# One decoder layer on one core: half a dense block more beside the first attention head, 640 keys cut as 320 and 320, and a norm's sum in two float32r parts

## The chip, the cores and the metric

The kernel runs on one core of a Trainium2 chip. The metric is device time of one execution in microseconds (us). The core has five engines with queues of their own: PE (TensorE, matrix products), DVE (VectorE), ACT (ScalarE), POOL (GpSimd) and SP, which here only issues DMAs. Each engine takes its instructions in program order and waits for others by semaphores.

## The reference

One layer of a decoder trunk on 1024 tokens of width 1024, all in float32:

```
u = rms_norm(h);  aq, ak, av, hq, hf, hi, hg = split(u @ w_in)
attn = rms_norm(dilated_attention(aq, ak, av))        # 8 heads of 64
rec  = rms_norm(hgrn2_mixer(hq, hf, hi)) * silu(hg)   # 4 heads of 128
h = h + concat(attn, rec) @ w_out
h = h + conv_glu(rms_norm(h));  return rms_norm(h)
```

The attention's three dilated branches are merged into one softmax by a mask that carries the logarithm of how many branches contain a pair of tokens. So a block of 128 queries at block number qb sees (qb + 1) * 128 keys, from 128 to 1024.

## The kernel before

**Numbers.** A float32 product is made of float32r parts: each operand is split into a high part (`hi`, a cast on ACT, L86 for weights) and the rest (`lo`, a subtraction, L88, on POOL or DVE), and PE makes three products, hi·hi, hi·lo and lo·hi. In the attention the weights' `lo` parts are made on POOL.

**Stages.** The projections of the first heads come first. Then the attention's eight heads run from about 50 to 298 us, the recurrent heads until about 500, then the output projection, the gated network and the last norm.

**One attention head.** Query blocks go in four pairs j = 0 to 3. `score_steps` makes the scores S of a block (L585, L586: q against the keys' high and low parts) in pieces of at most 512 keys, one per step. DVE adds the mask and takes the extreme (L588), with one more small operation where there are two pieces (L592). ACT takes the exponential (L593, tile P), DVE the reciprocal of its sum (L594), and POOL scales P by it, 512 columns at a time (L597). `value_steps` then transposes P on PE (L612 to L619, tile T), ACT and DVE split the result (L623, L624, tiles th and tl), and PE multiplies it with the values (L631 to L635, tile O; L639 and L641 add the two halves). The scores of pair j+1 are made while pair j is transposed, and the last pair of a head goes with the first pair of the next.

**S has two banks** (tag `s`). The third piece in a row may be written only once DVE has read the first.

**Fill.** Between these steps stand steps of other projections, so that PE has work while softmax goes through DVE, ACT and POOL. A step is three products: 512 columns wide for the queries and keys of a later head (`qk_half`, tile `p__qk_h_half`, eight steps each, L458 to L461) and for the recurrent part's tokens (`tok_pair`, tile piv, sixteen steps), 256 wide for values (tiles pV, L475 to L477 and L492 to L494). The list `beside[h]` names what stands beside head h. `cost[h]`/4 is the fill in planned us for each pair, shared evenly between its steps. What is left is run at the end of the head:

```python
share = cost[h] / 4 / (n_sc + n_va)
...
if got:
    fill.run(share)
```

PE's order is written out this way by hand. On DVE, ACT and POOL a scheduler sets the order when the program is built.

**Weights.** `Ring` holds five loaded weight pairs. `ring.done(key)` after a pair's last use frees a slot for the next pair's cast on ACT and its `lo` part on POOL. A projection of one query/key half uses two pairs, and the second half uses the same two and frees them. A value projection uses four.

**Attention norm.** `attn_norm` squares the heads' outputs and adds them in `acc` (L821 to L824), then sums over the partitions with a product against ones. This one is in plain float32:

```python
yield
ss = bank("t", f"ass{hf}")
PE.matmul(ss, ones, acc, start=True, stop=True)
R = rstd_part(acc, s2, ss, 1.0 / 512)
```

It runs twice, once for each half of the tokens, two units of the recurrent part's plan (5.2 planned us each) behind the squares. The norms before and after the gated network already use `parts_of` (ACT makes hi, DVE makes lo) and `sum_parts` (two float32r products, L344).

Of the kernel before, what the change touches and what calls it, by code (L numbers as in the profile page):

```python
# [14 lines left out]
ALU = mybir.AluOpType  # L15
# [6 lines left out]
H2 = 512  # L22
NH = 8
# [179 lines left out]
def hybrid_kernel(ctx: ExitStack, tc: tile.TileContext, xT, w_qk, w_tok, w_hg, w_out, w_up,  # L203
                  w_down, vecs, amask, hmask, out):
    nc = tc.nc
    PE, DVE, ACT, POOL = nc.tensor, nc.vector, nc.scalar, nc.gpsimd
# [128 lines left out]
    def parts_of(x, tile):  # L335

        hi, lo = tile("hi"), tile("lo")
        ACT.copy(hi, x)
        DVE.tensor_sub(lo, x, f32(hi))
        return hi, lo  # L340
# [142 lines left out]
    def two(kind, i, evac):  # L483

        key = f"{kind}_{i}"
        for e in range(2):
            o = bank("mm", f"p{key}_{e}")[:, :256]
            tk = slice((2 * i + e) * P, (2 * i + e + 1) * P)
            for c in range(NCT):
                hi, lo = ring.get((key, c // 2))  # L490
                s = slice((c % 2) * 256, (c % 2 + 1) * 256)
                PE.matmul(o, uhi[:, c, tk], hi[:, s], start=(c == 0), stop=False)  # L492
                PE.matmul(o, uhi[:, c, tk], lo[:, s], start=False, stop=False)
                PE.matmul(o, ulo[:, c, tk], hi[:, s], start=False, stop=(c == NCT - 1))  # L494
                if e and c % 2 == 1:
                    ring.done((key, c // 2))
                yield 0.33
            evac(2 * i + e, o)

    def tok_pair(i, evac, lag=2):  # L500

        ps = {}
        for k in range(NCT + lag):
            for e in range(2):
                c = k - e * lag
                if not 0 <= c < NCT:
                    continue
                if c == 0:
                    ps[e] = bank("mm", f"piv{i}_{e}")
                hi, lo = ring.get((("iv", i), c))  # L510
                tk = slice((2 * i + e) * P, (2 * i + e + 1) * P)
                PE.matmul(ps[e], uhi[:, c, tk], hi, start=(c == 0), stop=False)  # L512
                PE.matmul(ps[e], uhi[:, c, tk], lo, start=False, stop=False)  # L513
                PE.matmul(ps[e], ulo[:, c, tk], hi, start=False, stop=(c == NCT - 1))  # L514
                if e:
                    ring.done((("iv", i), c))
                yield 0.65
                if c == NCT - 1:
                    evac(2 * i + e, ps[e])
# [7 lines left out]
    if True:  # L527
# [30 lines left out]
        def qk_block(h):  # L558
            return [qk_half(h, 0, False), qk_half(h, 1, True)]

        def v_evac(g):
            def evac(t, ps):
                if g not in vs:
                    vs[g] = vtile([P, 8, 4, P], F32R, f"v{g}")
                dst = vs[g][:, t]
                src = ps[:, :256].rearrange("p (h e) -> p h e", h=4)
                ACT.mul(dst[:, :, 0:64], src, R1T[:, t : t + 1])
                DVE.scalar_tensor_tensor(dst[:, :, 64:128], src, R1T[:, t : t + 1], f32(dst[:, :, 0:64]),
                                         op0=ALU.mult, op1=ALU.subtract)
            return evac  # L570

        def score_steps(h, j):
            Ps = []
            qs, kh, kl = qk[h]
            for i in range(2):
                qb = 2 * j + i
                n = (qb + 1) * P
                Pt = at.tile([P, (5 + i + 2 * (j % 2)) * P], F32, tag=f"P{j % 2}{i}", name=f"P{h}_{qb}")
                st = at.tile([P, 16], F32, tag="st", name=f"st{h}_{qb}", bufs=8)
                Ps.append(Pt)  # L580
                for k0 in range(0, n, H2):
                    w = min(n, k0 + H2) - k0
                    S = bank("s", f"S{h}_{qb}_{k0}")
                    q = qs[:, qb * P : (qb + 1) * P]
                    PE.matmul(S[:, :w], q, kh[:, k0 : k0 + w], start=True, stop=False)  # L585
                    PE.matmul(S[:, :w], q, kl[:, k0 : k0 + w], start=False, stop=True)  # L586
                    m = SEQ - n + k0
                    DVE.tensor_tensor_reduce(Pt[:, k0 : k0 + w], S[:, :w], mask[:, m : m + w], -1.0, BIG * 3,  # L588
                                             op0=ALU.add, op1=ALU.min, accum_out=st[:, k0 // H2 : k0 // H2 + 1])
                    if k0 + w == n:  # L590
                        if k0:
                            DVE.tensor_tensor(st[:, 0:1], st[:, 0:1], st[:, 1:2], op=ALU.min)  # L592
                        ACT.activation(Pt[:, :n], Pt[:, :n], AF.Exp, bias=st[:, 0:1], scale=-1.0, accum_out=st[:, 2:3])  # L593
                        DVE.reciprocal(st[:, 3:4], st[:, 2:3])  # L594
                        for s0 in range(0, n, H2):
                            e = Pt[:, s0 : min(n, s0 + H2)]
                            POOL.tensor_scalar(e, e, st[:, 3:4], 1.0, op0=ALU.mult, op1=ALU.mult)  # L597
                    yield Ps
# [100 lines left out]
        for c in range(4):  # L699
# [2 lines left out]
        fill.add(v0[4])  # L702
        fill.run()
        ivs = [tok_pair(i, iv_evac) for i in range(4)]
        beside = {
            0: v0[5:] + [two("V1", 0, v_evac(1))],
            1: qk_block(2) + [two("V1", 1, v_evac(1))],
            2: qk_block(3) + [two("V1", 2, v_evac(1))],
            3: qk_block(4) + [two("V1", 3, v_evac(1))],
            4: qk_block(5) + [islice(ivs[0], 8)],  # L710
            5: [ivs[0]] + qk_block(6) + [islice(ivs[1], 8)],
            6: [ivs[1]] + qk_block(7) + [islice(ivs[2], 8)],
            7: [ivs[2], ivs[3]],
        }
        cost = {h: 4.8 * (4 if h in (5, 6) else 3) for h in range(NH)}
        cost[NH - 1] = 12.8
        for h in range(NH):
            fill.add(*beside[h])
# [46 lines left out]
    with pool("hg", "right") as hg:  # L765
# [52 lines left out]
        def attn_norm(hf):  # L818
            t = halves[hf]
            acc, s2 = gtile(f"asq{hf}"), gtile(f"asq{hf}_s")  # L820
            ACT.activation(acc, raw[0, hf], AF.Square)  # L821
            for c in range(1, 4):
                ACT.activation(s2, raw[c, hf], AF.Square)
                DVE.tensor_add(acc, acc, s2)  # L824
            yield
            ss = bank("t", f"ass{hf}")
            PE.matmul(ss, ones, acc, start=True, stop=True)
            R = rstd_part(acc, s2, ss, 1.0 / 512)
            yield
            for c in range(4):  # L830
                if c == 2:
                    yield
                a = raw[c, hf]
                DVE.scalar_tensor_tensor(a, a, col(V_AG + c), R, op0=ALU.mult, op1=ALU.mult)
                ACT.copy(attn_hi[:, c, t], a)
                DVE.tensor_sub(attn_lo[:, c, t], a, f32(attn_hi[:, c, t]))
            yield
# [695 lines left out]
```

## Time and profile before

| | |
|---|---|
| runs, us | 1208.57, 1209.03, 3102.54 |
| median, us | 1209.03 |
| profiled execution, us | 1207.86 |
| its span, first to last instruction, us | 1205.9 |
| granted TensorE clock, mean share of full speed | 0.998 |
| busy, share of the span: PE, PEld, DVE, ACT, POOL | 99%, 83%, 79%, 52%, 25% |

PE's busy time is modelled from pipelined products, so a busy PE may still lose some tenths of a us. How long a product really takes is read as the distance from one start to the next. One of the three runs stands far from the others, and the median does not hang on it.

### The profile page before, as it was taken

Reading aid. Unit: us, or ns where it says so; the run is one execution under the profiler, and the core shown is the slowest. Engines: PE = TensorE matmul, PEld = TensorE weight load, DVE = VectorE, ACT = ScalarE, POOL = GpSimd, SP = SyncE. Lnnn points to the kernel's source line nnn. Section 1 sums busy time; section 2 is a strip of 40 time slices with the busy share of each in tenths; the row PEclk is TensorE's granted clock in tenths of the full one; section 3 lists DMA queues with packets and bytes.
Section 4 is the critical chain, followed back from the end, with each engine's and each line's share of the span. In section 5 each row is a group of like instructions: output and inputs, shape, how many; then the busy total and the mean of one; then the engine's idle time right before and its main releaser. Section 6 shows DMA issues by size and latency. Waiting matters only on the chain.

```text
span 1205.9 us, 17474 instructions
## 1 busy us (share of the span) xinstructions
PE 1192.7 (99%) x6014; PEld 1005.6 (83%) x6014; DVE 947.8 (79%) x1783; ACT 631.4 (52%) x1217; POOL 298.5 (25%) x276
## 2 busy tenths in 40 slices
PE   9999999999999999999999999999999999999996
PEld 8988888888888888888888888888888888888886
DVE  8767776666778776484999899898888978957986
ACT  8766666667666565454643343433443444444553
POOL 1154446544001014413231322312223200000000
PEclk9999999999999999999999999999999999999999
DMA  7021112223111123432113323333223267534532
GB/s 273 10 71 54 53 54 88 64 65 120 36 36 54 60 64 112 133 125 94 42 64 114 108 85 106 121 116 109 84 98 122 96 213 249 156 98 158 166 103 89
DMA packets 71833, 122.39 MB, mean 101 GB/s; under 512 B 7360, under 2 KB 17856, under 8 KB 71744
## 3 DMA queue, kind: packets, MB, share of 16 engines
q1 hardware_dynamic: 60528, 101.41, 26.3%
q10 hardware_dynamic: 11216, 19.86, 4.3%
q8 instruction: 47, 0.77, 0.3%
q14 instruction: 42, 0.34, 0.1%
HBM read 97.65 MB, written 23.59 MB: 101 GB/s over the span
## 4 chain that ended last, share of the span: by engine, by line
PE 95%; DVE 3%; ACT 1%; issue 0%; POOL 0%; DVEq 0%; ACTq 0%
PE p L1132 11%; PE p L1133 11%; PE p L1134 11%; PE ds L1433 3%; PE ds L1431 3%; PE ds L1432 3%; PE po L1036 2%; PE po L1038 2%; PE po L1037 2%; PE da L1433 2%; PE da L1431 2%; PE da L1432 2%; PE piv L512 1%; PE piv L514 1%; PE piv L513 1%; PE S L585 1%
## 5 line engine op out<-in xcount | busy, mean ns | idle before, releaser
L88 POOL TENSOR_TENSOR wlo<-raww,whi 128x512 fp32r<-128x512 f32 x141 | 208.6, 1491 | 382.4 <-ACT whi L86 231.6
L86 ACT CAST whi<-raww 128x512 fp32r<-128x512 f32 x276 | 167.7, 617 | 183.9 <-DVE raww L120 69.1
L88 DVE TENSOR_TENSOR wlo<-raww,whi 128x512 fp32r<-128x512 f32 x136 | 97.5, 717 | 22.8 <-ACT whi L86 22.7
L86 ACT CAST whi<-r 128x512 fp32r<-128x512 f32 x70 | 43.6, 623 | 83.1 <-PE ds L1432 51.3
L597 POOL TENSOR_SCALAR P<-P,st 128x512 f32<-128x512 f32 (+2 forms) x96 | 55.8, 592 | 107.9 <-DVE st L594 50.5
L588 DVE CUSTOM_DVE_ANT_0 P<-S,mask 128x512 f32<-128x512 f32 (+2 forms) x96 | 52.0, 553 | 29.9 <-PE S L586 28.9
L593 ACT ACTIVATE P<-P,st 128x128 f32<-128x128 f32 (+3 forms) x64 | 49.7, 777 | 32.0 <-DVE st L588 16.7
L88 DVE TENSOR_TENSOR wlo<-r,whi 128x512 fp32r<-128x512 f32 x70 | 47.9, 685 | 20.0 <-ACT whi L86 19.9
L624 DVE TENSOR_TENSOR tl<-T,th 128x512 fp32r<-128x512 f32 (+1 forms) x80 | 50.8, 634 | 16.2 <-ACT th L623 15.1
L1433 PE MATMUL ds<-fhi,wlo 128*128 128x512 f32 x160 | 62.3, 389 | 0.0
L1432 PE MATMUL ds<-flo,whi 128*128 128x512 f32 x160 | 62.3, 389 | 0.0
L1431 PE MATMUL ds<-fhi,whi 128*128 128x512 f32 x160 | 62.2, 389 | 0.0
L1132 PE MATMUL p<-b1h,whi 128*128 128x512 f32 x160 | 62.2, 389 | 0.0
L1133 PE MATMUL p<-b1l,whi 128*128 128x512 f32 x160 | 62.2, 389 | 0.0
L1134 PE MATMUL p<-b1h,wlo 128*128 128x512 f32 x160 | 62.2, 389 | 0.0
L1161 ACT ACTIVATE cv<-cv 128x512 f32<-128x512 f32 x44 | 27.9, 633 | 61.5 <-DVE cv L1154 61.4
L1154 DVE SCALAR_TENSOR_TENSOR cv<-g,vec,cv 128x511 f32<-128x511 f32 (+2 forms) x92 | 56.1, 615 | 4.7 <-ACT cv L1151 3.7
L1405 POOL TENSOR_TENSOR facc<-facc,sqf 128x256 f32<-128x256 f32 x2 | 1.5, 738 | 223.7 <-ACT sqf L1404 223.7
L623 ACT CAST th<-T 128x512 fp32r<-128x512 f32 (+1 forms) x80 | 43.0, 537 | 23.4 <-PE T L616 20.3
L86 ACT CAST fhi<-rawf 128x512 fp32r<-128x512 f32 x70 | 43.2, 617 | 15.2 <-DMA rawf<-spT 7.0
L88 DVE TENSOR_TENSOR flo<-rawf,fhi 128x512 fp32r<-128x512 f32 x70 | 47.9, 684 | 3.6 <-ACT fhi L86 3.6
L1431 PE MATMUL da<-fhi,whi 128*128 128x512 f32 x120 | 46.7, 389 | 0.0
(672 smaller groups left out, 3832.5 us busy)
## 6 DMA issues: line engine op xcount, KB each, us to landing
raww<-in_w_up_dram SPq DMA_DIRECT2D x88, 256.0 KB, 3.1
raww<-in_w_tok_dram SPq DMA_DIRECT2D x52, 256.0 KB, 2.7
rawf<-spT SPq DMA_DIRECT2D x40, 256.0 KB, 2.7
r<-in_w_down_dram SPq DMA_DIRECT2D x40, 256.0 KB, 3.5
raww<-in_w_hg_dram SPq DMA_DIRECT2D x32, 256.0 KB, 2.6
raww<-in_w_out_dram SPq DMA_DIRECT2D x32, 256.0 KB, 2.6
spB<-a ACTq DMA_DIRECT2D x30, 256.0 KB, 2.2
spT<-t ACTq DMA_DIRECT2D x30, 256.0 KB, 2.0
```

The costliest lines, as they stand in the source:

```text
L86: self.pin(self.high(hi[:, :w], raw))
L88: self.pin(low.tensor_sub(lo[:, :w], raw, f32(hi[:, :w])))
L588: DVE.tensor_tensor_reduce(Pt[:, k0 : k0 + w], S[:, :w], mask[:, m : m + w], -1.0, BIG * 3, op0=ALU.add, op1=ALU.min, accum_out=st[:, k0 / ...
L597: POOL.tensor_scalar(e, e, st[:, 3:4], 1.0, op0=ALU.mult, op1=ALU.mult)
L624: DVE.tensor_sub(tl[:, :n], T[:, :n], f32(th[:, :n]))
L1132: PE.matmul(ps, hi[:, s], bhi, start=(start and n == 0), stop=False)
L1133: PE.matmul(ps, hi[:, s], blo, start=False, stop=False)
L1134: PE.matmul(ps, lo[:, s], bhi, start=False, stop=(stop and n == len(rhs) - 1))
L1154: DVE.scalar_tensor_tensor(dst, x, col(V_CW + j * NFF + f), dst, op0=ALU.mult, op1=ALU.add)
L1431: PE.matmul(ps[d], hi[:, s], ahi, start=(k == 0), stop=False)
L1432: PE.matmul(ps[d], hi[:, s], alo, start=False, stop=False)
L1433: PE.matmul(ps[d], lo[:, s], ahi, start=False, stop=(k == NPAIR - 1))
```

## The change

Three edits.

1. A block with 640 keys was cut in 512 and 128. It is now cut in 320 and 320 (`cut`). Every head has one such block (qb = 4).
2. `beside` is shifted by half a query/key block from head 0 to head 4. Head 0 gets the first half of head 2's block, and heads 1 to 3 run the second half of one block, a value projection and the first half of the next block. Head 4 gets the second half of head 5's block and the whole first token pair. Head 5 loses what head 0 won (half a token pair's place), so that from head 6 on all stands as before. The sequence of the fill is the same as before. What changes is which score and value steps it stands between. Head 0's planned cost goes from 14.4 to 17.3 us, head 5's from 19.2 to 14.4.
3. `attn_norm` makes high and low parts of `acc`, in the not yet used space of `attn_hi` and `attn_lo`, and sums these with two float32r products.

```diff
-                for k0 in range(0, n, H2):
-                    w = min(n, k0 + H2) - k0
+                cut = 320 if n == 640 else H2
+                for k0 in range(0, n, cut):
+                    w = min(n, k0 + cut) - k0
...
-            0: v0[5:] + [two("V1", 0, v_evac(1))],
-            1: qk_block(2) + [two("V1", 1, v_evac(1))],
+            0: v0[5:] + [two("V1", 0, v_evac(1)), blocks[2][0]],
+            1: [blocks[2][1], two("V1", 1, v_evac(1)), blocks[3][0]],
...
-        cost = {h: 4.8 * (4 if h in (5, 6) else 3) for h in range(NH)}
+        cost = {h: 4.8 * {0: 3.6, 6: 4}.get(h, 3) for h in range(NH)}
...
+
+            parts = parts_of(acc, lambda x: (attn_hi if x == "hi" else attn_lo)[:, 0, t])
             yield
             ss = bank("t", f"ass{hf}")
-            PE.matmul(ss, ones, acc, start=True, stop=True)
+            sum_parts(ss, parts)
```

What this does to the order of instructions is shown at three places.

POOL in head 0, pairs 1 and 2, before and then with the change. P_4 to P_7 are the softmax blocks, wlo the low parts of weights; a block's number stands behind its name, and the last number is the buffer's.

```order
L597 TENSOR_SCALAR P_4_659<-P_4_659,st_4_660 128x512
L597 TENSOR_SCALAR P_4_659<-P_4_659,st_4_660 128x128
L88 TENSOR_TENSOR wlo_751<-raww_748,whi_750 128x512
L597 TENSOR_SCALAR P_5_703<-P_5_703,st_5_704 128x512
L597 TENSOR_SCALAR P_5_703<-P_5_703,st_5_704 128x256
L88 TENSOR_TENSOR wlo_781<-raww_778,whi_780 128x512
```

```order
L598 TENSOR_SCALAR P_4_662<-P_4_662,st_4_663 128x512
L598 TENSOR_SCALAR P_4_662<-P_4_662,st_4_663 128x128
L88 TENSOR_TENSOR wlo_739<-raww_736,whi_738 128x512
L88 TENSOR_TENSOR wlo_759<-raww_756,whi_758 128x512
L88 TENSOR_TENSOR wlo_775<-raww_772,whi_774 128x512
L598 TENSOR_SCALAR P_5_709<-P_5_709,st_5_710 128x512
L598 TENSOR_SCALAR P_5_709<-P_5_709,st_5_710 128x256
```

Three low parts instead of one now stand between block 4 and block 5.

ACT at the same place, before and then with the change: exponentials (L593, then L594), casts of weights (whi), casts of transposed blocks (th), a value projection's result (v) and the copy of O (ot).

```order
L593 ACTIVATE P_4_659,st_4_660<-P_4_659,st_4_660 128x640
L623 CAST th_1_1_728<-T_1_1_724 128x384
L567 ACTIVATE v_436<-pV_6_655,R1T 128x4x64
L639 COPY ot_0_754<-O_0_638 64x256
L86 CAST whi_750<-raww_748 128x512
L593 ACTIVATE P_5_703,st_5_704<-P_5_703,st_5_704 128x768
L86 CAST whi_780<-raww_778 128x512
```

```order
L594 ACTIVATE P_4_662,st_4_663<-P_4_662,st_4_663 128x640
L567 ACTIVATE v_436<-pV_6_655,R1T 128x4x64
L86 CAST whi_738<-raww_736 128x512
L624 CAST th_1_1_749<-T_1_1_745 128x384
L86 CAST whi_758<-raww_756 128x512
L640 COPY ot_0_778<-O_0_641 64x256
L594 ACTIVATE P_5_709,st_5_710<-P_5_709,st_5_710 128x768
L86 CAST whi_774<-raww_772 128x512
```

Two weight casts instead of one stand ahead of block 5's exponential, and the third cast, which POOL's third low part needs, stands behind it.

PE in head 1, from block 6's second piece of scores to block 7's first, before and then with the change.

```order
L586 MATMUL S_6_512_1171<-kl_206,qs_319 128x384
L458 MATMUL p__qk___2_1_1115<-uhi,whi_945 128x512
L460 MATMUL p__qk___2_1_1115<-ulo,whi_945 128x512
L461 MATMUL p__qk___2_1_1115<-uhi,wlo_946 128x512
L612 MATMUL T_2_0_1184<-ident,P_4_1069 128x128
L613 MATMUL T_2_0_1184<-ident,P_5_1100 128x128
L615 MATMUL T_2_0_1184<-ident,P_4_1069 128x128
L616 MATMUL T_2_0_1184<-ident,P_5_1100 128x128
L585 MATMUL S_7_0_1195<-kh_320,qs_319 128x512
```

```order
L587 MATMUL S_6_512_1221<-kl_206,qs_319 128x384
L492 MATMUL pV_1_1_1232<-whi_925,uhi 128x256
L493 MATMUL pV_1_1_1232<-wlo_926,uhi 128x256
L494 MATMUL pV_1_1_1232<-whi_925,ulo 128x256
L613 MATMUL T_2_0_1237<-ident,P_4_1109 128x128
L614 MATMUL T_2_0_1237<-ident,P_5_1146 128x128
L616 MATMUL T_2_0_1237<-ident,P_4_1109 128x128
L617 MATMUL T_2_0_1237<-ident,P_5_1146 128x128
L492 MATMUL pV_1_1_1232<-whi_925,uhi 128x256
L493 MATMUL pV_1_1_1232<-wlo_926,uhi 128x256
L494 MATMUL pV_1_1_1232<-whi_925,ulo 128x256
L586 MATMUL S_7_0_1257<-kh_320,qs_319 128x512
```

A step of the value projection now stands between the transposition T_2_0 and the scores S_7_0, where nothing stood. Heads 2 and 3 have the same order as head 1. In head 0 there are 24 steps of fill between the scores S_2 and the transposition T_2_0, where there were 20.

## Rows read from the trace of the kernel before

**Rows 1.** The page's first part: PE's and the other engines' busy time, share of the span and number of instructions.

```profile
PE 1192.7 (99%) x6014; PEld 1005.6 (83%) x6014; DVE 947.8 (79%) x1783; ACT 631.4 (52%) x1217; POOL 298.5 (25%) x276
```

**Rows 2.** Busy time by stretch: start and end, length, then busy time and instructions of PE, PEld, DVE, ACT and POOL, the granted clock, DMA share and GB/s. The stretches are about head 0, head 1 and head 5.

```profile
50.00:79.00 29.00, 27.26 (x208) 25.83 (x207) 21.07 (x61) 22.62 (x49) 17.72 (x21) 1.00 0.22 66
79.00:106.00 27.00, 26.62 (x179) 23.98 (x179) 19.74 (x54) 17.79 (x38) 10.82 (x15) 1.00 0.09 29
...
201.00:237.00 36.00, 36.00 (x202) 30.76 (x201) 22.82 (x59) 23.77 (x50) 20.28 (x24) 1.00 0.26 77
```

**Rows 3.** What PE waited for in the whole span: us in total, times, the longest.

```profile
PE T L613 <- POOL P L597: 1.7, 2, 1.1
...
PE S L585 <- DVE st L588: 0.8, 2, 0.4
```

**Rows 4.** PE's instructions in head 0 around its two waits, in order of time: start, duration, line, tile, and in brackets the idle time before it and what ended it.

```profile
52.81 0.27 PE L612 MATMUL T<-ident,P 128*128 128x128 f32 x1
53.67 0.33 PE L613 MATMUL T<-ident,P 128*128 128x128 f32 x1 [0.60 <-POOL P L597]
...
59.21 0.28 PE L475 MATMUL pV<-whi,uhi 128*128 128x256 f32 x1
...
59.57 0.27 PE L612 MATMUL T<-ident,P 128*128 128x128 f32 x1
...
60.98 0.33 PE L613 MATMUL T<-ident,P 128*128 128x128 f32 x1 [1.14 <-POOL P L597]
```

**Rows 5.** ACT and POOL at the same place, in order of time for each: exponentials (L593), weight casts (L86), scaling (L597) and low parts (L88).

```profile
56.71 0.48 ACT L623 CAST th<-T 128x384 fp32r<-128x384 f32 x1 [0.29 <-PE T L619]
...
57.84 0.37 ACT L639 COPY ot<-O 64x256 f32<-64x256 f32 x1 [0.28 <-PE O L635]
...
58.78 0.93 ACT L593 ACTIVATE P<-P,st 128x768 f32<-128x768 f32 x1
...
59.77 0.62 ACT L86 CAST whi<-raww 128x512 fp32r<-128x512 f32 x1
...
52.93 0.69 POOL L597 TENSOR_SCALAR P<-P,st 128x512 f32<-128x512 f32 x1 [2.23 <-DVE st L594]
...
58.96 1.29 POOL L88 TENSOR_TENSOR wlo<-raww,whi 128x512 fp32r<-128x512 f32 x1 [0.82 <-ACT whi L86]
60.23 1.15 POOL L597 TENSOR_SCALAR P<-P,st 128x512 f32<-128x512 f32 x2
```

**Rows 6.** PE's score products of head 1 with 128, 512 and 384 columns, with the instruction that follows each.

```profile
82.53 0.22 PE L585 MATMUL S<-kh,qs 128*128 128x128 f32 x1
82.59 0.28 PE L586 MATMUL S<-kl,qs 128*128 128x128 f32 x1
82.70 0.30 PE L612 MATMUL T<-ident,P 128*128 128x128 f32 x1
...
88.82 0.39 PE L586 MATMUL S<-kl,qs 128*128 128x512 f32 x1
89.05 0.34 PE L585 MATMUL S<-kh,qs 128*128 128x384 f32 x1
...
89.40 0.39 PE L458 MATMUL p__qk___2_1_1115<-uhi,whi 128*128 128x512 f32 x1
```

**Rows 7.** The first scores of block 7 behind the last products of T_2_0, in heads 1, 2 and 3, and DVE's reading of block 6's first scores in head 1.

```profile
90.32 0.27 PE L615 MATMUL T<-ident,P 128*128 128x128 f32 x1
90.43 0.27 PE L616 MATMUL T<-ident,P 128*128 128x128 f32 x1
91.08 0.50 PE L585 MATMUL S<-kh,qs 128*128 128x512 f32 x1 [0.38 <-DVE st L588]
...
90.33 0.69 DVE L588 CUSTOM_DVE_ANT_0 P<-S,mask 128x512 f32<-128x512 f32 x1
...
120.96 0.27 PE L616 MATMUL T<-ident,P 128*128 128x128 f32 x1
121.37 0.50 PE L585 MATMUL S<-kh,qs 128*128 128x512 f32 x1
...
151.20 0.27 PE L616 MATMUL T<-ident,P 128*128 128x128 f32 x1
151.86 0.50 PE L585 MATMUL S<-kh,qs 128*128 128x512 f32 x1 [0.38 <-DVE st L588]
```

**Rows 8.** The attention norm's sum of the first half (tile ass) with what follows on PE, the two-part sum of a later norm (tile ss), and the last addition of squares ahead of the first.

```profile
303.46 0.69 DVE L824 TENSOR_TENSOR asq<-asq,asq_s 128x512 f32<-128x512 f32 x1 [0.70 <-ACT asq_s L823]
...
310.73 1.02 PE L827 MATMUL ass<-asq,ones 128*128 128x512 f32 x2
311.19 0.80 PE L458 MATMUL p__hq___0_0_3895<-uhi,whi 128*128 128x512 f32 x1
311.82 0.39 PE L460 MATMUL p__hq___0_0_3895<-ulo,whi 128*128 128x512 f32 x1
...
518.23 0.40 PE L344 MATMUL ss<-acchi,ones 128*128 128x512 f32 x1
...
518.71 0.40 PE L1036 MATMUL po<-rec_hi,whi 128*128 128x512 f32 x1
```

**Rows 9.** Busy time and granted clock at the end of the span, columns as in rows 2.

```profile
1198.00:1200.00 2.00, 0.00 (x0) 0.00 (x0) 1.93 (x6) 0.12 (x1) 0.00 (x0) 1.00 0.93 329
1200.00:1203.00 3.00, 0.00 (x0) 0.00 (x0) 2.76 (x7) 0.00 (x0) 0.00 (x0) 0.53 0.63 224
```

More of the change, by code (lines that the diff above doesn't have):

```diff
@@ L588, in score_steps @@
                     DVE.tensor_tensor_reduce(Pt[:, k0 : k0 + w], S[:, :w], mask[:, m : m + w], -1.0, BIG * 3,
-                                             op0=ALU.add, op1=ALU.min, accum_out=st[:, k0 // H2 : k0 // H2 + 1])
+                                             op0=ALU.add, op1=ALU.min, accum_out=st[:, k0 // cut : k0 // cut + 1])
                     if k0 + w == n:
@@ L704, in hybrid_kernel @@
         ivs = [tok_pair(i, iv_evac) for i in range(4)]
+        blocks = {h: qk_block(h) for h in range(2, NH)}
         beside = {
-            0: v0[5:] + [two("V1", 0, v_evac(1))],
-            1: qk_block(2) + [two("V1", 1, v_evac(1))],
[L708 to L712, printed above, removed]
+            0: v0[5:] + [two("V1", 0, v_evac(1)), blocks[2][0]],
+            1: [blocks[2][1], two("V1", 1, v_evac(1)), blocks[3][0]],
+            2: [blocks[3][1], two("V1", 2, v_evac(1)), blocks[4][0]],
+            3: [blocks[4][1], two("V1", 3, v_evac(1)), blocks[5][0]],
+            4: [blocks[5][1], ivs[0]],
+            5: blocks[6] + [islice(ivs[1], 8)],
+            6: [ivs[1]] + blocks[7] + [islice(ivs[2], 8)],
             7: [ivs[2], ivs[3]],
         }
-        cost = {h: 4.8 * (4 if h in (5, 6) else 3) for h in range(NH)}
+        cost = {h: 4.8 * {0: 3.6, 6: 4}.get(h, 3) for h in range(NH)}
         cost[NH - 1] = 12.8
```

## The prediction

> **What bounds the kernel now.** I read the busy times first. PE is busy for 1192.7 of the 1205.9 us [rows 1], so only two things can shorten this kernel: fewer columns on PE, or less idle time of PE. Next comes PE's list of waits, because it is short: in the whole span PE waits twice for POOL's scaling of P, 1.7 us together, and twice for DVE's reading of scores, 0.8 us [rows 3]. The stretches say where. Head 0 lacks 1.7 of 29 us, head 1 lacks 0.4 of 27, and head 5 lacks nothing of 36 [rows 2]. Last I look at single instructions by their starts, since a duration of a pipelined product overlaps the next one. In head 0 the second product of a transposition starts 0.86 behind the first at 52.81, and 1.41 behind it at 59.57 [rows 4]. A transposition's product takes 0.11 when nothing is in the way (90.32 to 90.43 [rows 7]), so these two cost 0.75 and 1.30. In heads 1, 2 and 3 the scores of block 7 start 0.65, 0.41 and 0.66 behind the last product of T_2_0 [rows 7]; less 0.11 each, that is 0.54, 0.30 and 0.55. DVE reads the scores that hold the bank from 90.33 on, 0.69 long, and PE goes on at 91.08 [rows 7].
>
> So the edits can touch about 3.4 us of idle time and a few products. 2% of this kernel, about what a measurement of it can tell from no change, is 24 us.
>
> **640 keys as 320 and 320.** Removed in each of eight heads: two products of 512 columns and two of 128. A 512 takes 0.23 (88.82 to 89.05), and the two of 128 take 0.17 together (82.53 to 82.70), more than their share of columns [rows 6]. That is 0.63. Added: four products of 320. The trace has none. Two of 384 take 0.35 (89.05 to 89.40 [rows 6]), so 0.175 each; by columns a 320 takes 0.146, and four take 0.58. The gain is 0.05 in a head, **0.4 in all**, and it counts in full because PE is the bound. From both sides: if a 320 costs what a 384 does, four take 0.70 and the edit loses 0.5 in all; if it costs what a 256 does, 0.12 by the step of three from 59.21 to 59.57 [rows 4], it gains 1.2. I take the value by columns, since 512 and 384 lie on one line (0.45 and 0.46 ns for a column). DVE reads the same 640 columns in two pieces as before. Nothing new waits there.
>
> **The norm's sum in two parts.** From the start of the old sum to the second product behind it are 1.09 us (310.73 to 311.82 [rows 8]). One product of 512, 0.23, is in that, so the sum takes 0.86. The later norm's two parts take 0.48 (518.23 to 518.71 [rows 8]). The gain is 0.38 for each half, **0.76 in all**. Float32 taken apart so costs 0.86/0.23 = 3.7 of a float32r product. The Trainium skill ("FP8 and Floating Point Precision", TensorE Precision Notes) says that true FP32 takes four passes through the array; the trace comes near, and by the page the old sums would cost 0.92 each and the gain would be 0.88. I stay with the rows. New are a cast on ACT (0.62, as the weight cast [rows 5]) and a subtraction on DVE (0.69, as the one for squares [rows 8]) ahead of each sum. The squares are ready at 304.15 (303.46 + 0.69) and PE wants the sum at 310.73 [rows 8]; 1.3 us of new work lies inside 6.6 us. Cost nothing. What hides it is the two units of the plan between the steps; without that cover it would be 1.3 for each half. On DVE the next thing queued behind the wait for the cast is the recurrent gate's arithmetic, and the subtraction stands one instruction behind the squares, so DVE waits at most 0.6 there, and PE waits nowhere for DVE in this stage [rows 3].
>
> **Head 0.** The order shows 24 steps of fill instead of 20 ahead of T_2_0. A step of three takes 0.36 (59.21 to 59.57 [rows 4]), so PE arrives at T_2_0 with 4 x 0.36 = 1.4 us more work done. Three of these steps stand ahead of the first wait. P's block 3 is ready on POOL at 53.62 (52.93 + 0.69 [rows 5]); what DVE, ACT and POOL do before it is in the old order, and PE comes there about 1.07 later than 52.81, that is 53.9. **The first wait, 0.75, goes.** The second does not. POOL takes three low parts ahead of block 5, not one, and the third needs a weight cast that ACT makes only after block 5's exponential. Worked through: the exponential started at 58.78 with 0.29 and 0.28 of idle time among the instructions ahead of it [rows 5]; one more cast of 0.62 now stands there, so it starts at about 59.0. The next cast started 0.99 behind it (58.78 to 59.77) and takes 0.62: 60.6. The third low part takes 1.29: 61.9. Block 5's first 512 columns take 0.69 as block 3's did [rows 5]: 62.6. PE may then go on with T_2_0 at 62.65, where it went on at 60.98. It has waited about 2.3 us, more than both waits together before. Since 1.4 us more work is done by then, head 0 as a whole loses 62.65 - 60.98 - 1.4, **about 0.3**. From both sides: if block 5 comes in time, head 0 gains the whole 2.05; if it comes one low part later still, it loses 1.6.
>
> **Heads 1 to 4.** From S_2 to T_2_0 each of these heads has as many fill steps as before, and DVE and ACT have the same evacuation of a query/key half in the middle, so DVE should read block 6's first scores at the same place. What changes is that one value step, 0.36, stands between T_2_0 and S_7_0 in heads 1 to 3. Of 0.54, 0.30 and 0.55 there remain 0.18, 0 and 0.19: **a gain of 1.0**. Two more weight casts now stand ahead of block 5's exponential on ACT in these heads, but POOL's blocks 4 and 5 come ahead of the parts of the third and later ones. Head 4's order at this place stays as it was. **Head 5** had enough fill to lose nothing [rows 2]. It now has the fill and the order that heads 1 to 3 had before, two query/key halves and no step behind T_2_0. I give it their wait, between 0.30 and 0.55: **a loss of 0.45**. Bounds for both together: a gain of 1.4 (all the waits go, none comes) and a loss of 1.1 (none goes, head 5 gets twice the wait).
>
> **The sum.** -0.4 - 0.76 + 0.3 - 1.0 + 0.45 = -1.4 us. The profiled execution took 1207.86, so it would take 1206.5. The median of the runs shown, 1209.03, is 1.2 above it, and my forecast is for such a median: **1207.6**.
>
> **Rivals.** *The extra fill does its work in head 0.* Then both waits go, 2.05 instead of a loss of 0.3: 1205.3. For it: the first wait surely has too little work in front of it. Against it: the second wait is POOL's queue, and fill on PE brings nothing forward there; more fill even frees weights earlier for POOL to work on. Chance 0.18.
>
> *POOL's queue repeats in heads 1 to 3.* The new order puts two low parts ahead of block 4 in each of these heads, where four stood in one row behind block 1. The second part's cast waits until PE has finished a query/key half. If blocks 4 and 5 come late for T_2_0 by it, each head loses up to one part, 1.29 [rows 5]. At half of that in three heads, 1.9, the total is 1209.5, and the change is slower than before. It decides from 1.4 us on, that is about 0.5 us of late arrival in each head. Against it: the cast falls in a stretch where ACT idles before block 4's exponential, and PE's list has no wait of these heads for POOL [rows 3]. Chance 0.13.
>
> *The clock falls in head 0.* PE's idle stretch of 1.14 us passed at a clock of 1.00 [rows 2, 4]. At the end of the span two us without any product still show 1.00, and the three behind them show 0.53, the way to 1.2 of 2.4 GHz [rows 9]. A wait of 2.3 us in head 0 lies between. If the clock falls there, products take twice as long until it is back. The trace does not show how long that is. Between nothing and the rest of head 0 (79 less 61 us at half speed, 9 us lost) I take 4: 1211.6. The Trainium skill ("TensorE: Matmul & The Clock Gate", Why this matters for your kernels) advises against idle gaps between bursts of matmuls because the array falls back to its lower clock. [...] Chance 0.06.
>
> **How the numbers follow.** The forecast has 0.63, the rivals 0.18, 0.13 and 0.06. The forecast's own terms reach from about -2.6 to +0.3 when two bounds fall together, that is 1206.4 to 1209.3. The range takes in the first two rivals, and leaves the clock out: 1205.2 to 1210.0. No case comes near 24 us, so faster by over 2% gets 0.01, slower 0.02 for what no row shows, and within 2% 0.97.
>
> **What would show it.** Right: the products of tile ass come as two with 0.48 to the next; scores of 320 columns stand 0.15 apart; the wait of T for POOL at about 54 is gone and the one at about 60 lasts over 2 us; heads 1 to 3 show no idle time before S_7_0 and head 5 does. Wrong: a head 0 without idle time (the first rival), new waits of T for POOL in heads 1 to 3 (the second), or a clock under 1.00 behind 60 us (the third). The forecast is wrong above all if POOL's order on the chip costs less than I worked out by hand from single rows, because ACT and POOL have slack that I did not see.

## The result, and the profile after

The changed kernel takes 1214.28 us (median of six runs, 1213.48 to 1214.80) where the kernel before, run beside it, takes 1208.67. The ratio is 1.0046, with a 95% interval of 1.0035 to 1.0057. It is slower by 5.6 us. The prediction was 1207.6 with a range up to 1210.0, so sign, size and range were wrong. The profiled execution took 1214.80 (before 1207.86), and its 6.9 us are the sum that I take apart below.

PE's busy time first, the answer to [rows 1], then its waits, the answer to [rows 3]:

```profile
PE 1195.2 (99%) x6014; PEld 1008.6 (83%) x6014; DVE 955.2 (79%) x1785; ACT 631.1 (52%) x1219; POOL 299.0 (25%) x276
```

```profile
PE T L614 <- POOL P L598: 2.8, 1, 2.8
PE S L586 <- DVE st L589: 2.1, 6, 0.6
PE T L613 <- DVE tl L625: 2.0, 4, 0.6
```

One wait for POOL where there were two, but longer than both together. The scores wait for DVE six times, not twice. A wait is there that the kernel before did not have: transpositions T for DVE's low parts tl. And DVE, with two instructions more, is busy 7.4 us longer than before. That last number led to the cause.

Head 0 by stretch (columns as in [rows 2]):

```profile
60.00:62.00 2.00, 0.54 (x5) 0.31 (x3) 1.75 (x6) 1.79 (x4) 1.52 (x2) 1.00 0.53 143
62.00:63.30 1.30, 0.00 (x0) 0.00 (x0) 0.63 (x1) 0.58 (x1) 1.30 (x3) 0.72 0.57 183
63.30:69.40 6.10, 6.06 (x25) 5.68 (x26) 2.80 (x8) 2.03 (x5) 2.90 (x4) 0.50 0.23 86
69.40:80.00 10.60, 10.60 (x86) 10.29 (x86) 5.28 (x15) 7.89 (x19) 7.25 (x8) 1.00 0.19 67
```

PE stands idle, and 2.0 us after its last product has ended (60.54 to 62.57) the granted clock falls to 0.50, 1.2 of 2.4 GHz. It stays there for 6.1 us after PE has gone on. The same place on PE, ACT, DVE and POOL (the answer to [rows 4, 5]; start, duration, and in brackets the idle time before and what ended it):

```profile
59.74 0.94 ACT L594 ACTIVATE P<-P,st 128x768 f32<-128x768 f32 x1 [0.91 <-DVE st L593]
60.67 1.12 ACT L86 CAST whi<-raww 128x512 fp32r<-128x512 f32 x2
...
58.88 0.76 DVE L593 TENSOR_TENSOR st<-st 128x1 f32<-128x1 f32 x1
...
58.33 2.54 POOL L88 TENSOR_TENSOR wlo<-raww,whi 128x512 fp32r<-128x512 f32 x2
61.35 1.26 POOL L88 TENSOR_TENSOR wlo<-raww,whi 128x512 fp32r<-128x512 f32 x1 [0.48 <-ACT whi L86]
62.59 1.15 POOL L598 TENSOR_SCALAR P<-P,st 128x512 f32<-128x512 f32 x2
...
60.27 0.27 PE L613 MATMUL T<-ident,P 128*128 128x128 f32 x1
63.34 0.47 PE L614 MATMUL T<-ident,P 128*128 128x128 f32 x1 [2.80 <-POOL P L598]
...
65.32 0.63 PE L586 MATMUL S<-kh,qs 128*128 128x512 f32 x1
65.74 0.63 PE L587 MATMUL S<-kl,qs 128*128 128x512 f32 x1
```

Three low parts stand ahead of block 5, as the order had shown. What no one had reckoned with is the DVE line. The small minimum of a block's two extremes, two columns of 128x1, took 0.16 in most places before. Here it takes 0.76, beside a low part on POOL, and ACT idles 0.91 until it is done and block 5's exponential can start. About 0.6 of that is the longer minimum. At half clock the two scores of 512 columns start 0.42 apart, where [rows 6] have 0.23.

The minima of the whole kernel, before and then after (duration min/median/max in ns):

```profile
L592 DVE TENSOR_TENSOR st<-st x32: 150/160/1102, 55.2 to 284.5; 128x1 f32<-128x1 f32 x32
```

```profile
L593 DVE TENSOR_TENSOR st<-st x32: 159/182/1260, 55.5 to 292.5; 128x1 f32<-128x1 f32 x32
```

By line they sum to 8.1 us before and 15.6 after. That is 7.4 more, as much as DVE's whole increase; the other changes on DVE are each at most 1.5 us, some up and some down. Thirteen of the minima take over 0.5, where three did before (1.10, 1.09 and 0.61, in heads 5 to 7), and each of the thirteen ends within 0.02 us of a POOL instruction that had begun before it. At the end of head 2 it looks so:

```profile
135.13 1.26 DVE L593 TENSOR_TENSOR st<-st 128x1 f32<-128x1 f32 x1
138.23 0.69 DVE L625 TENSOR_TENSOR tl<-T,th 128x512 fp32r<-128x512 f32 x1 [0.30 <-ACT th L624]
...
135.09 1.28 POOL L88 TENSOR_TENSOR wlo<-raww,whi 128x512 fp32r<-128x512 f32 x1 [1.83 <-ACT whi L86]
...
136.48 1.16 ACT L594 ACTIVATE P<-P,st 128x1024 f32<-128x1024 f32 x1 [1.47 <-DVE st L593]
137.63 0.56 ACT L624 CAST th<-T 128x512 fp32r<-128x512 f32 x1
...
141.67 0.56 ACT L624 CAST th<-T 128x512 fp32r<-128x512 f32 x1
...
142.27 0.69 DVE L625 TENSOR_TENSOR tl<-T,th 128x512 fp32r<-128x512 f32 x1
...
139.06 0.30 PE L613 MATMUL T<-ident,P 128*128 128x128 f32 x1 [0.38 <-DVE tl L625]
143.02 0.33 PE L613 MATMUL T<-ident,P 128*128 128x128 f32 x1 [0.63 <-DVE tl L625]
```

POOL starts a low part at 135.09 and ends it at 136.37. DVE's minimum starts at 135.13 and ends at 136.39: it lasts just as long as POOL's instruction. Block 7's exponential comes late by that, the casts of transposed blocks queue behind it on ACT, tl is late on DVE, and the transpositions of the last pair wait for the bank that tl still reads.

**Where the 6.9 us are.** For each product of PE I took the distance to the next start, less the median distance that the same pair of shapes has in the kernel before (pairs with 320 columns, which it lacks, against their own median), and summed this by stretch in both kernels. A head's stretch goes from its first scores to the next head's, so it holds the last pair of the head before. Ahead of head 0 the changed kernel lost 0.3 more than the kernel before, head 0 up to the end of its wait 0.7, the rest of head 0, with the half clock, 2.7, head 1 0.3, head 2 0.5, head 3 1.5, head 4 1.8, head 5 0.5, heads 6 and 7 nothing. That is 8.0 before rounding. Behind the heads it gives 1.1 back, 0.8 of it in the norm's two sums: 7.0.

### The profile page after: what moved, and what is told of

Read it like the earlier page. It is cut to its first block, busy times and chain, and to the rows that moved or that the text cites. A ratio compares the mean times of both kernels' runs of the same rounds, so it can differ in the third digit from the quotient of the medians.

```text
span 1212.9 us, 17490 instructions
## 1 busy us (share of the span) xinstructions
PE 1195.2 (99%) x6014; PEld 1008.6 (83%) x6014; DVE 955.2 (79%) x1785; ACT 631.1 (52%) x1219; POOL 299.0 (25%) x276
## 4 chain that ended last, share of the span: by engine, by line
PE 92%; DVE 4%; issue 1%; POOL 1%; ACT 1%; DVEq 0%; ACTq 0%; POOLq 0%
PE p L1138 10%; PE p L1137 10%; PE p L1136 10%; PE ds L1436 3%; PE ds L1435 3%; PE ds L1437 3%; PE po L1040 2%; PE po L1042 2%; PE po L1041 2%; PE da L1436 2%; PE da L1435 2%; PE da L1437 2%; PE piv L512 1%; PE piv L514 1%; PE piv L513 1%
## 5 line engine op out<-in xcount | busy, mean ns | idle before, releaser
L88 POOL TENSOR_TENSOR wlo<-raww,whi 128x512 fp32r<-128x512 f32 x141 | 209.0, 1491 | 394.5 <-ACT whi L86 229.0
L86 ACT CAST whi<-raww 128x512 fp32r<-128x512 f32 x276 | 167.5, 616 | 179.8 <-DVE raww L120 68.0
L88 DVE TENSOR_TENSOR wlo<-raww,whi 128x512 fp32r<-128x512 f32 x136 | 97.5, 718 | 25.0 <-ACT whi L86 24.8
L86 ACT CAST whi<-r 128x512 fp32r<-128x512 f32 x70 | 43.6, 623 | 83.7 <-PE ds L1436 50.0
L589 DVE CUSTOM_DVE_ANT_0 P<-S,mask 128x512 f32<-128x512 f32 (+3 forms) x96 | 52.0, 551 | 20.9 <-PE S L587 20.6
L594 ACT ACTIVATE P<-P,st 128x128 f32<-128x128 f32 (+3 forms) x64 | 49.7, 777 | 33.9 <-DVE st L593 22.7
L88 DVE TENSOR_TENSOR wlo<-r,whi 128x512 fp32r<-128x512 f32 x70 | 48.0, 686 | 19.4 <-ACT whi L86 19.4
L88 DVE TENSOR_TENSOR flo<-rawf,fhi 128x512 fp32r<-128x512 f32 x70 | 48.0, 685 | 4.6 <-ACT fhi L86 4.6
L86 ACT CAST fhi<-rawf 128x512 fp32r<-128x512 f32 x70 | 43.1, 616 | 14.1 <-DMA rawf<-spT 6.1
```

The source lines that it names most:

```text
L86: self.pin(self.high(hi[:, :w], raw))
L88: self.pin(low.tensor_sub(lo[:, :w], raw, f32(hi[:, :w])))
```

## The experiments

**The cut alone** (the kernel before with `cut`).

```diff
-                for k0 in range(0, n, H2):
+                cut = 320 if n == 640 else H2
+                for k0 in range(0, n, cut):
```

> The kernel before with the cut of 640 keys into 320 and 320 alone. By the working of the prediction a head saves 0.05 us on PE, so the time goes down by 0.4 us, with bounds of +0.5 and -1.2. If the cut itself made the change slower (a longer second piece of scores that DVE reads later), this kernel is slower than before by more than 0.5 us and shows waits of the scores for DVE in block 4 that the kernel before does not have.

Measured: 1210.33, ratio 1.0014 (1.0005 to 1.0023): slower by 1.7. The products cost what was forecast: in the changed kernel 320 columns start 0.145 apart (90.53, 90.67, 90.82). Nor does block 4 wait. The loss is in head 0, at block 5:

```profile
54.40 0.69 DVE L549 TENSOR_TENSOR x<-p__qk___1_1_273,R 128x512 f32<-128x512 f32 x1
...
59.16 0.94 ACT L594 ACTIVATE P<-P,st 128x768 f32<-128x768 f32 x1 [0.44 <-DVE st L593]
...
60.09 0.60 ACT L86 CAST whi<-raww 128x512 fp32r<-128x512 f32 x1
...
60.77 1.26 POOL L88 TENSOR_TENSOR wlo<-raww,whi 128x512 fp32r<-128x512 f32 x1 [1.72 <-ACT whi L86]
62.02 1.14 POOL L598 TENSOR_SCALAR P<-P,st 128x512 f32<-128x512 f32 x2
...
62.76 0.33 PE L614 MATMUL T<-ident,P 128*128 128x128 f32 x1 [2.65 <-POOL P L598]
```

The kernel before has two of these at other places:

```profile
52.07 0.69 DVE L549 TENSOR_TENSOR x<-p__qk___1_1_273,R 128x512 f32<-128x512 f32 x1
...
58.25 0.62 ACT L86 CAST whi<-raww 128x512 fp32r<-128x512 f32 x1
```

PE's order changed only in the pieces, but the scheduler then ordered the other engines anew: head 1's query/key evacuation starts at 54.40 on DVE where it started at 52.07, and ACT casts the weight at 60.09, behind block 5's exponential, where the cast stood ahead of it at 58.25. POOL's low part starts at 60.77 where it started at 58.96. Neither of my two expectations had this. The eleven executions stand in two groups: four at 1209.17 to 1209.54, seven at 1210.31 to 1211.76, with a mean clock of 0.996 in six of the seven and 0.997 or 0.998 in the others. In the profiled one, the fastest, the clock stays at 1.00 behind the 2.65 us. That it fell in the seven is argued from their mean clock; none of them was traced.

**The norm alone.** The edit of the change, third part.

> The kernel before with the attention norm's sum in two float32r parts alone. By the working of the prediction each of two sums takes 0.48 us in place of 0.86, so the time goes down by 0.76 us. If the new cast and subtraction stand in the way of other work on ACT or DVE, the gain is smaller, or the time goes up.

Measured: 1207.50, ratio 0.9989 (0.9980 to 0.9998), faster by 1.1. In the changed kernel's trace the two parts stand as forecast, 0.48 from the first to the product behind (the answer to [rows 8]):

```profile
318.74 0.40 PE L344 MATMUL ass<-attn_hi,ones 128*128 128x512 f32 x1
318.98 0.40 PE L344 MATMUL ass<-attn_lo,ones 128*128 128x512 f32 x1
319.22 0.40 PE L458 MATMUL p__hq___0_0_3897<-uhi,whi 128*128 128x512 f32 x1
```

**The shifted fill alone** (`beside` and `cost` of the change).

> The kernel before with the shifted fill alone. My theory now is that the whole loss is in this edit: head 0's longer wait for POOL, half clock behind it, and new waits in heads 1 to 5. By the medians the change lost 5.6 us, and the two other edits should have won 1.2, so this kernel should be slower than before by 6.5 to 7 us, with a granted clock of 0.50 for some us behind 62 us. The rival, that two edits hurt only together (a 320 cut that moves DVE's reading against the new fill), gives a loss of under 4 us here.

Measured: 1215.27, ratio 1.0051 (1.0038 to 1.0063), slower by 6.6. The waits are those of the whole change: POOL 2.7, scores 2.1 (six), tl 1.9 (four), and the clock stands at 0.52 from 64.5 to 68 us, just behind PE's going on at 64.00. So the loss is in the shift. With it the cut costs nothing more, since head 0 waits for three low parts anyway; its 1.7 and the others' losses don't add.

**What the clock costs.** The changed kernel, with products that do nothing in the idle time.

```diff
                 T = bank("t", f"T{h}_{j}_{i}")
+                if (h, j, i) == (0, 2, 0):
+                    for _ in range(12):
+                        PE.matmul(T, uhi[:, 0, 0:P], uhi[:, 0, 0:H2], start=True, stop=True)
```

> The changed kernel with twelve more products of 512 columns ahead of the transposition T_2_0 of head 0, written into T's own bank, which T then overwrites: they fill the 2.8 us in which PE stood idle, and do nothing for the result. Twelve at 0.23 us are 2.76 us, so PE reaches P's block 5 when it did before. If the idle time is what lets the clock fall, the clock stays at 1.00 there and the time goes down by what the half clock cost, 2.6 us of start-to-start excess between 63.3 and 70 us: about 1211.7 where the changed kernel has 1214.3. If the clock falls for another reason (the weights' DMAs at that place, or an allowance for the whole program), it falls here too and the time stays within 0.5 us of the changed kernel's. The waits of the later heads should stay as they are by either.

Measured: 1212.34, ratio 1.0030 (1.0019 to 1.0042). The profiled execution took 1212.21, 2.6 less than the changed kernel's; by the medians it is 1.9. The waits in later heads are unchanged (2.3 and 1.9). Columns as above:

```profile
62.00:63.00 1.00, 1.00 (x6) 0.84 (x5) 0.93 (x1) 0.07 (x1) 1.00 (x2) 1.00 0.50 131
63.00:70.00 7.00, 6.89 (x54) 6.32 (x53) 3.76 (x11) 4.67 (x10) 4.65 (x7) 1.00 0.26 95
```

POOL's order is the same, ACT's and DVE's differ only in two evacuations behind 64 us, and the DMAs are there as before. Only PE isn't idle: the idle time lets the clock fall, and it costs 1.9 to 2.6 us.

**Without the minimum.** The second piece's reduction starts from the first piece's result.

```diff
-                    DVE.tensor_tensor_reduce(..., mask[:, m : m + w], -1.0, BIG * 3,
+                    DVE.tensor_tensor_reduce(..., mask[:, m : m + w], -1.0, st[:, 0:1] if k0 else BIG * 3,
...
-                            DVE.tensor_tensor(st[:, 0:1], st[:, 0:1], st[:, 1:2], op=ALU.min)
```

> The changed kernel without the small minimum: the second piece of a block's scores takes the first piece's extreme as the starting value of its own reduction, so the operation on DVE between two 128x1 columns is gone in all 32 places. In the changed kernel these 32 took 15.6 us against 8.1 before, and eleven of them lasted until the end of an instruction that POOL was running. If this stop beside POOL is what makes DVE late (my theory), the four waits of the transpositions for tl in heads 3 and 4 (1.9 to 2.0 us) go, the waits of S_7_0 in heads 1 to 3 shrink by 0.5 each, and the time falls by 3 us or more, to about 1211. If the waits come from wide fill steps that leave no work between the transpositions (the rival), they stay at 0.5 and 0.8 and the time falls by under 0.7. Head 0's wait for POOL should stay over 2.5 us by either, with the fall of the clock.

Measured: 1206.34, ratio 0.9982 (0.9973 to 0.9991): 7.9 below the changed kernel and faster than before. More than expected, because head 0's wait went down too, to 1.1, and the clock stayed at 1.00. But the scheduler had also made another order, and in it POOL takes block 5 ahead of the third low part. So I kept the operation and changed its form alone.

**The minimum with one tensor.**

```diff
-                            DVE.tensor_tensor(st[:, 0:1], st[:, 0:1], st[:, 1:2], op=ALU.min)
+                            DVE.tensor_scalar(st[:, 0:1], st[:, 0:1], st[:, 1:2], BIG * 3, op0=ALU.min, op1=ALU.min)
```

> The changed kernel with the small minimum in another form: the second piece's extreme comes as a per-partition scalar operand of a tensor-scalar operation, not as a second tensor. The operation stays at its place on DVE, and ACT's and POOL's orders stay as they are, but for two casts on ACT around T_2_2 of head 0's last-but-one pair and for POOL's third low part in head 0, which now stands behind block 5. If the stop beside POOL belongs to an operation with two tensors in SBUF (my theory), the 32 minima take 0.16 us each, 5.2 in all where they took 15.6, the waits of the transpositions for tl in heads 3 and 4 go, and the time comes within 1 us of the kernel without the minimum (1206.34). If the gain of that kernel came from the other order of DVE and ACT that it also had, the waits in heads 3 and 4 stay and the time stays at 1209 or more, since here only head 0's order of POOL differs.

Measured: 1206.22, ratio 0.9984 (0.9975 to 0.9993), 8.1 below the changed kernel. The 32 minima, and PE's waits:

```profile
L593 DVE TENSOR_SCALAR st<-st x32: 194/214/215, 55.6 to 283.7; 128x1 f32<-128x1 f32 x32
```

```profile
PE S L586 <- DVE st L589: 1.6, 5, 0.4
PE T L614 <- POOL P L598: 1.1, 1, 1.1
...
128.95 0.21 DVE L593 TENSOR_SCALAR st<-st 128x1 f32<-128x1 f32 x1
...
128.92 1.29 POOL L88 TENSOR_TENSOR wlo<-raww,whi 128x512 fp32r<-128x512 f32 x1 [0.80 <-ACT whi L86]
```

No minimum takes over 0.215, though the same places stand beside POOL: at 128.95 it starts 0.03 behind a low part, as at 135.13 in the changed kernel, and takes 0.21 where it took 1.26. In all they take 6.8 us, more than the 5.2 that I expected and far less than 15.6. The waits for tl are gone, with ACT's and POOL's orders of heads 2 to 5 as they were and DVE's different only in where two reciprocals stand. The reciprocals are not the reason: the late tl of the changed kernel starts at 142.27, as soon as the cast that it needs has ended (141.67 + 0.56). That settles the waits for tl. By the spacing, heads 1 to 5 together lose 0.3 more here than in the kernel before, where the changed kernel lost 4.4. In head 0 the third low part went behind block 5 here too, so the runs don't tell how its gain divides between the minimum (0.6 on the way to the exponential) and the place of that low part (1.3).

**Head 0's low parts on DVE.**

```diff
+        ring.on_vector += [("V1_0", i) for i in (1, 2, 3)]
```

> The changed kernel with the low parts of weights 1 to 3 of the first later value projection made on DVE in place of POOL. These are the three that stand ahead of block 5 on POOL in head 0. By my theory POOL's queue is the second wait: without it block 5 is ready some 3 us earlier on POOL, less what DVE's three subtractions of 0.7 us delay its own reading, so the wait of T_2_0 shrinks from 2.8 us to under 1.5, the clock stays at 1.00 and the time falls by 3 to 5 us. If DVE, which is 97% busy from 50 to 60 us, is the limit there, the wait only moves to DVE's side and the time falls by less than 2. The later heads stay as they are by either.

Measured: 1211.15, ratio 1.0022 (1.0013 to 1.0032), 3.1 below the changed kernel (profiled 1211.12, 3.7 below). The wait is 1.60 instead of 2.80, and 1.00 is granted throughout. So the edit is worth 1.2 at the wait and 2.6 in the clock. The 1.2 can't be put down to POOL's queue alone: with no low part beside it, block 5's minimum takes 0.15 here. In the 1.60 that remain DVE has its part, since block 5's reciprocal comes at 61.16 behind two of the low parts, and POOL then takes 1.00 for the first 512 columns, beside the third low part, where it takes 0.69 in the kernel before.

**The same without the minimum.**

> The changed kernel without the small minimum and with the low parts of weights 1 to 3 of the first later value projection on DVE. Without the minimum one wait for POOL is left in head 0, 1.1 us, behind two low parts on POOL. If POOL's queue is that wait, it goes below 0.6 and the time falls from 1206.34 to about 1205.7. If DVE, with two or three more subtractions of 0.7 us ahead of block 5's reading, is as late as POOL was, the wait stays and the time stays at 1206.3 or rises.

Measured: 1206.51, ratio 0.9985 (0.9976 to 0.9993): no gain over 1206.34. POOL has nothing ahead of block 5 now, and idles 2.10 us:

```profile
60.24 1.46 POOL L597 TENSOR_SCALAR P<-P,st 128x512 f32<-128x512 f32 x2 [2.10 <-PE pV L477]
...
59.32 0.68 DVE L88 TENSOR_TENSOR wlo<-raww,whi 128x512 fp32r<-128x512 f32 x1
59.92 0.16 DVE L594 RECIPROCAL st<-st 128x1 f32<-128x1 f32 x1
60.00 0.69 DVE L88 TENSOR_TENSOR wlo<-raww,whi 128x512 fp32r<-128x512 f32 x1
```

DVE has taken POOL's place: the reciprocal, whose sum ACT has ready at 59.46, waits for the low part from 59.32, POOL takes 1.01 for its first 512 columns beside the next one, and PE still waits 1.0.

**The old fill without the minimum**, with the norm in parts, and then with the cut too.

> The kernel before with the norm's sum in two parts and without the small minimum. By my theory the minimum costs little in the kernel before, since only three of its 32 stood beside a running POOL instruction for over 0.5 us, in heads 5, 6 and 7, where PE did not wait: the gain over the norm alone (1207.5) is what DVE's time is worth in heads 1 and 3, where S_7_0 waits for DVE, under 1 us. So 1206.7 to 1207.5. If the order that the scheduler makes for head 0 changes for the worse, as it did with the 320 cut, the time is 1208 or more.

> The same with the cut of 640 keys into 320 and 320 too. The cut alone lost 1.7 us because the new order of DVE and ACT around it made block 5 of head 0 1.5 us later, and that in turn let the clock fall in some executions. If this is a matter of the order that the scheduler finds, which is another one without the minimum, the cut may cost nothing here or win its 0.4; if it comes from the second piece of scores itself, head 0 waits over 2 us again and the time stands 1.5 us over the kernel without the cut.

Measured: 1207.54 (0.9992, 0.9983 to 1.0001) and 1206.17 (0.9981, 0.9972 to 0.9990). Without the cut the minimum's removal wins nothing over the norm alone (1207.50): PE's waits for DVE are gone, but it waits six times for POOL, 3.6 together. With the cut it is 1.4 lower, so the cut's loss was a matter of the order that the scheduler found. The kernel with the cut and the two with the new fill and no stopped minimum (1206.34, 1206.22) are the fastest here, and the same within what is measured: all beat both kernels, and the shift is worth nothing in them.

**What S_7_0 still waits for.** The cast of the keys to ACT, with the new fill, then with the old one.

```diff
-                (ACT.copy if h < 2 else DVE.tensor_copy)(kh[0:64, t], x[64:128])
+                ACT.copy(kh[0:64, t], x[64:128])
```

> The changed kernel with the minimum in its scalar form, and with one more operation off DVE: the cast of a query/key half's keys for heads 2 to 7 (0.42 to 0.67 us, twelve times) goes to ACT, where heads 0 and 1 have it already. What is left over in that kernel are waits of S_7_0 for DVE's reading of block 6 in heads 1 to 5, about 0.28 in three of them and 0.38 in two by the list of waits, 1.6 together. My theory is that DVE is late there because the evacuation of the half stands ahead of the reading and is itself stopped beside POOL: then some 0.6 less on DVE takes these waits away in heads 1 to 3 and most of them in heads 4 and 5, and the time falls by 1 to 1.6 us from 1206.22. The rival: DVE waits in turn for ACT's cast (the subtraction that follows needs it), or ACT's exponentials become late. Then the waits stay or move to POOL's scaling, and the time stays or rises.

> The same two edits of DVE's work with the 320 cut and the norm in two parts, but with the fill where the kernel before has it. The kernel with the old fill and no minimum took 1206.17, with waits of 1.4 us for POOL in head 0 and 0.8 for DVE in heads 1 and 3. If the shift is worth nothing once DVE is not stopped, this comes within 0.5 us of the run beside it; if the shift helps when DVE is free, as the prediction reckoned for heads 1 to 3, this is slower by 0.5 to 1 us.

Measured: 1208.17 (0.9994, 0.9985 to 1.0003) and 1207.55 (0.9989, 0.9980 to 0.9998). My theory fell, and the rival holds: the waits of S_7_0 rose from 1.6 to 3.0. In the first of the two, head 1:

```profile
92.09 0.63 ACT L552 CAST kh<-x 64x512 fp32r<-64x512 f32 x1
92.74 0.94 ACT L594 ACTIVATE P<-P,st 128x768 f32<-128x768 f32 x1
...
93.80 0.16 DVE L595 RECIPROCAL st<-st 128x1 f32<-128x1 f32 x1 [0.56 <-ACT P L594]
95.73 0.69 DVE L589 CUSTOM_DVE_ANT_0 P<-S,mask 128x512 f32<-128x512 f32 x1
```

DVE idles for block 5's exponential, because the reciprocal of its sum stands ahead of the reading of block 6 in DVE's order. The cast put 0.6 more ahead of that exponential on ACT. What makes DVE late for block 6 without the cast stays open. The kernel with the old fill, 1207.55, is 0.6 below the other, so again not the slower one.

## Why the prediction was wrong, point by point

Three steps failed. The half clock, which the sum had at nothing, cost 2.7 us by the spacing. Heads 1 to 5, forecast to win 0.55, lost 4.4: minima on DVE were stopped beside POOL's moved work, which the forecast did not price, and with the minimum in its scalar form the same heads lose 0.3. And the cut, taken as free of any new wait, reordered the other engines in head 0.

**640 keys as 320 and 320.** The term on PE was right (0.145 for 320 columns). The step that failed is "Nothing new waits there". Only PE's order is written by hand; the other engines are ordered when the program is built, and a smaller second piece moved DVE, ACT and POOL in head 0. Alone: +1.7 instead of -0.4. I had the orders to compare, and compared them only where the fill moved.

**The norm.** Right: 0.48 for 0.86, 1.1 us by the medians against 0.76.

**Head 0.** The mechanism was right. The first wait went (the second product at 54.07, 0.11 behind the first), the second grew behind three low parts. I let PE go on at 62.65; it was 63.34. Of the missing 0.7, 0.6 is the minimum's 0.76 in place of 0.16, just ahead of the exponential that I had put at 59.0 and that came at 59.74.

**The clock.** This rival happened, with a price of 2.6 in the profile where I took 4, and I gave it 0.06. That chance contradicted my own rows: I forecast a wait of 2.3 us, and [rows 9] had a clock of 1.00 for two us without products and 0.53 over the next three. By these rows a wait of just that length should have had about an even chance. The whole trace would not have settled it: PE's last product had ended at 1196.71, so the clock there fell after 3.5 us of idle time, in head 0 of the changed kernel after 2.0, and in the kernel with the shifted fill alone only when PE, after 2.73 us, had gone on. The sentence of the Trainium skill that I cited against idle gaps ("TensorE: Matmul & The Clock Gate", Why this matters for your kernels) bears here in head 0 too: idle times of 1.14 and 1.60 us passed at 1.00, 2.65 did in the one execution that was traced, and 2.73 and 2.80 cost the clock.

**Heads 1 to 4.** I expected 1.0 us less. By the spacing that I had used, 0.47, 0.44 and 0.47 are left at S_7_0 in heads 1 to 3 of 0.54, 0.30 and 0.55, so nothing was won there, and the second product of T_2_0 comes 0.25 to 0.30 later. The ends of heads 2 and 3 (the stretches of heads 3 and 4 above) have the new waits for tl, 2.0 together, which no rival named, at a place that I had not looked at: the last pair, where I knew that the fill's steps change from narrow to wide. Width was not the cause, since the waits went with the same order on PE. The failed step is "DVE should read block 6's first scores at the same place". I worked DVE through by durations from a trace in which POOL's low parts lay elsewhere. In heads 1 to 3 the change put a low part ahead of block 4's scaling, which so came to stand beside block 5's minimum: 0.54. It put another beside block 6's minimum (1.19 to 1.21), and in heads 2 and 3 one beside block 7's: 1.26. The stops are not the whole of it. Without them the waits for tl are gone and T_2_0 comes in time, but S_7_0 still waits 0.28 in each of heads 1 to 3; why DVE reads late there stays open.

The Trainium skill has the rule ("SBUF — State Buffer", Who interferes with whom): an instruction of DVE with two inputs in SBUF contends with an instruction of GpSimd that reads SBUF, and the one that comes later stands still until the other is done. The traces agree: 1.26 for two 128x1 columns, ending with POOL's instruction, and 0.21 with one tensor input. They agree on the other side as well: the subtraction of tl, whose first input lies in PSUM, never takes over 0.69 in 80 instructions, thirteen of which start within a low part on POOL. In the kernel before, rows of such stops were there to read, 1.10 us for a minimum in head 5 the longest, but PE did not wait for them.

**Heads 4 and 5.** Head 5 got about the wait that I gave it: 0.38 idle, 0.55 by the spacing, for 0.45. In head 4, of which I said that its order stays, S_7_0 starts 0.90 behind the last product of T_2_0, where it started 0.41 behind it.

**The rival of POOL's queue in heads 1 to 3** was half right: the waits of T_2_0 for POOL came, at 0.3 a head and not 1.29. The work that it delayed was DVE's.

## What to carry to other kernels

Where two engines share something, a moved instruction is priced with its new neighbours: before moving POOL's work, list what DVE does with two SBUF inputs beside its new place, down to the 128x1 operations, and give those another form first. A change of a hand-written order changes the orders that a scheduler makes of it, so compare all engines, and not only where the edit lies. And a single idle time of PE as long as those here, 2.7 us, is to be priced with the clock behind it, or filled with products that do nothing.

## What the runs showed of the hardware

- A minimum of two 128x1 columns in SBUF took up to 1.26 us on DVE beside a POOL subtraction of 128x512, and 0.54 beside a POOL scaling. With the second column as a scalar operand it took 0.194 to 0.215 in 32 of 32 places, thirteen of which had taken over 0.5. The kernel with this one operand changed was 8.1 us faster; in it one low part of head 0 also stood elsewhere on POOL.
- PE's clock fell to 0.50 in the changed kernel during an idle time of 2.80 us and came back 6.1 us after PE had gone on. With the shifted fill alone it fell 0.7 us after the end of an idle time of 2.73 and came back 4.1 us after that end. After 2.65 us it stayed at 1.00 in the one execution that was traced.
- Twelve idle-time products kept the clock at 1.00 with POOL, DVE, ACT and the DMAs at nearly the same work.
